# Filler work around 64 attention heads: from one generator with two calls per step to tasks placed by a planner

## The chip, the cores and the metric

The kernel runs on one core of a Trainium2 chip. The metric is the device time of one execution in microseconds (us). The core has TensorE (PE, matrix products and transposes into PSUM), VectorE (DVE), ScalarE (ACT), GpSimd (POOL) and SyncE (SP, which here issues the DMAs). Each engine works through its own instructions strictly in the order in which the program emits them, and an instruction waits on semaphores for operands that another engine makes.

## The reference

One layer of a hybrid backbone: 128 context tokens and 1024 latent tokens, model width 1024. Cut to what matters here:

```python
h = rmsnorm(x, norm1_w) * (1 + sc1) + sh1
aq, ak, av, mq, mk, mv, mo, mg = split(h @ w_in)      # 8 query heads, 2 key/value heads, 64 wide
attn_o = softmax(aq @ keys^T / 8) @ vals              # latent queries: 1024 latent + 128 context keys
hm = rmsnorm(mlstm(mq, mk, mv, gates)) * sigmoid(mo)
x = x + g1 * (concatenate([attn_o, hm]) @ w_out)
h2 = rmsnorm(x, norm2_w) * (1 + sc2) + sh2
g, u = split(h2 @ w_gu)                               # each 2816 wide
x = x + g2 * ((silu(g) * u) @ w_down)
y = rmsnorm(x, final_norm_w)
```

## The kernel before

The tokens stand in nine tiles of 128: tile `b = 0` is the context, `b = 1..8` are latent. The program has four stages, one after the other: modulation, first norm, input projection and the mLSTM heads; the attention stage; gate and up projection, in 22 pieces of 128 columns, with the down projection; the last norm. The change is all in the attention stage, which lies between about 437 and 838 us, and in the few microseconds after it.

**The attention stage** is a loop over `step(n)`, one step for each of 64 heads (8 latent tiles with 8 query heads), and some steps after the last head. The instructions of a head are spread over the engines, and in step `n`:

- PE computes the scores of head `n+2` into PSUM (`S<-kst,qT`, L1106; two halves of PSUM alternate, so they can only start once the exp of head `n` has read its half). On odd steps it also computes the values of the pair of heads that ended before (`po<-phT` and `po<-plT`, L1049, 18 products).
- DVE takes the reciprocal of head `n`'s sum (L1443) and scales it (L1444), finds the maximum of head `n+1` (`st<-S`, L1110), and makes the low half of head `n`'s probabilities (`pl`, L1454). Probabilities and weights are held as a high and a low half, so that two or three products give nearly f32.
- ACT makes the high half (`ph<-pr,st`, L1446), which needs DVE's scale, then the exp of head `n+1` (`pr<-S,st`, L1114), which needs DVE's maximum, and on odd steps copies the values out (`ol<-po`, L1054 and L1055).
- SP issues the transposing DMAs of both halves (L1450, L1455). POOL adds the two halves of the output (`oT`) and the gated residual (`x<-x,t`, L1132).

**The fillers** are all other work of this stage: the query projection of tiles 3 to 8 with its norm and rotary part (`q_part`), the turning of queries (`turn_products`, `turn_copies`), the splitting of `w_out` into a high and a low half (`out_load`, `out_split`), the mLSTM half of the output projection (`hm_part`), and the attention half with the second norm (`out_part`, `norm_stats`, `norm_rows`, `norm_turn`, `norm_out`). One piece of a projection (`out_block`, half a tile) is 12 products of 512 columns, and `add_gated` adds it to the residual `x1`. Before, one generator, `filler()`, walks through all of it in a fixed order, and a step calls it twice: the first `next(fill)` lets it emit a PE portion ahead of the values, the second, at the end of the step, the matching ACT and DVE instructions. So an ACT instruction and the DVE instruction that reads its result are emitted in the same step:

```python
def out_split(raw, tags):       # ACT cast, then DVE difference
    ...
    nc.scalar.copy(hi, raw)
    sub(lo, raw, hi.bitcast(F32), "dve")
```

After the last head come three more steps, the rest of the generator, and then the first gate/up piece, `pieces[0]`: its two 128x1024 weight tiles are loaded, measured (`measure`, L1522: a sum of squares on ACT), summed over the partitions (`scales`, one product with ones, L1527, and eight small DVE instructions), and split into two half-precision parts (`convert`: `wpair` on ACT, L1544, and its remainder on DVE, L1545). `split_down` does the like for `w_down`, piece by piece (`wdt`).

Of the kernel before, what the change touches and what calls it, by code (L numbers as in the profile page):

```python
# [19 lines left out]
P = 128  # L20
D = 1024
# [24 lines left out]
def hybrid_step(ctx: ExitStack, tc: tile.TileContext, I: dict, O: dict):  # L46
# [610 lines left out]
    def norm_rope_steps(qp, cc, ss, x, nb, nh, w, rb, eng=dve):  # L657
# [5 lines left out]
        act(sq, xf, AF.Square)  # L663
        ssum = qp.tile([P, 16], F32, name=nm("nrs"), tag="nrs", bufs=1)[:, :n]
# [358 lines left out]

    def turn_copies(b, ps):
        qT = qTs[b] = ap.tile([P, NQ, P], F32R, name=nm("qT"), tag="qT", bufs=2)
        psv = ps.rearrange("p (j x) -> p j x", j=4)
        qv = qT.rearrange("p (j g) x -> p j g x", g=2)
        for g in range(2):
            own = slice(64 * g, 64 * g + 64)
            far = slice(64 - 64 * g, 128 - 64 * g)  # L1030
            nc.scalar.copy(qv[own, :, g, :], psv[own])
            sub(qv[far, :, g, :], psv[own], qv[own, :, g, :].bitcast(F32), "dve")

    def new_oT(b):
        if b == 0:
            return half2[:, 5].rearrange("p (k x) -> p k x", k=4)
        if b in (3, 4):
            return hq.tile([P, 4, P], F32, name=f"o{b}")
        return ap2.tile([P, 4, P], F32, name=nm("oT"), tag="oT", bufs=3)
# [156 lines left out]
    def out_load(half, i):  # L1196
        n, j = divmod(i, 2)
        r0 = half * 512 + 2 * j * P
        raw = wp.tile([P, 1024], F32, name=nm("raw"), tag="raw", bufs=2)
# [25 lines left out]
    def q_part(state):  # L1225

        ropes = []
        raws, ws = [], []
        jobs = {1: lambda: raws.append(out_load(1, 0)), 2: lambda: raws.append(out_load(1, 1)),
                4: lambda: (ws.append(out_split(raws[0], ("wlo", "wlo"))), raws.append(out_load(1, 2))),  # L1230
                6: lambda: (ws.append(out_split(raws[1], ("wlo", "wlo"))), raws.append(out_load(1, 3))),
                8: lambda: ws.append(out_split(raws[2], ("wlo", "whi")))}
        s = 0
        for b in range(CB, NB):
            c, i = divmod(b, CB)
            sl = slice(i * P, (i + 1) * P)
            for half in range(2):
                if half == 0:
                    ps = bank()
                for k in range(4 * half, 4 * half + 4):  # L1240
                    wh, wl = w_q[k // 2]
                    ah, al = hTh[c][:, k, sl], hTl[c][:, k, sl]
                    mm(ps, ah, wh[:, k % 2, :], start=(k == 0), stop=False)
                    mm(ps, ah, wl[:, k % 2, :], start=False, stop=False)
                    mm(ps, al, wh[:, k % 2, :], start=False, stop=(k == KD - 1))
                yield 1
                if half == 1:
                    r = ev_rest(b, ps)
                    if r is not None:
                        ropes.append(r)  # L1250
                if ropes and next(ropes[0], ropes) is ropes:
                    ropes.pop(0)
                if s in jobs:
                    jobs[s]()
                s += 1
                yield
        while ropes:
            yield 0
            if next(ropes[0], ropes) is ropes:
                ropes.pop(0)  # L1260
            if len(ws) == 3:
                ws.append(out_split(raws[3], ("whi", "whi")))
            yield
        state["ws"] = [ws[0:2], ws[2:4]]

    def hm_part(ws):

        def load_hm(b):
            hm = t2()
            dma(hm, hm_d[b * P : (b + 1) * P, :])  # L1270
            return hm

        def load_x1(b):
            dma(x1[b], xrow(b))

        ring = [hq.tile([P, 2, 4, P], F32R, name=f"ring{i}") for i in range(2)]
        load_x1(0)
        hms = {0: load_hm(0)}
        raws = []
        for b in range(-1, NB):  # L1280
            for n in range(2):
                if b < 0 and n == 0:
                    continue
                if b >= 0:
                    th, tl = (ring[b % 2][:, t] for t in range(2))
                    ps = out_block(ws, n, th, tl)
                turn = b + 1 < NB and (n == 0 or b < 0)
                if turn:
                    pt = bank()
                    hm = hms.pop(b + 1)  # L1290
                    for j in range(4):
                        transpose(pt[:, j * P : (j + 1) * P], hm[:, j * P : (j + 1) * P])
                yield (b >= 0) + turn
                if b >= 0:
                    add_gated(x1[b], ps, gx[n] if b == 0 else gs[n], n, pool)
                if turn:
                    psv = pt.rearrange("p (j x) -> p j x", j=4)
                    oh, ol = (ring[(b + 1) % 2][:, t] for t in range(2))
                    nc.scalar.copy(oh, psv)
                    sub(ol, psv, oh.bitcast(F32), "dve")  # L1300
# [3 lines left out]
                    if b < 0:  # L1304
                        load_x1(1)
# [508 lines left out]
```

## Time and profile before

| quantity | value |
|---|---|
| median of 3 runs | 1655.72 us (1654.65 to 1659.19) |
| the profiled execution | 1659.14 us, its span 1657.4 us |
| mean granted clock of PE | 0.95 |
| PE busy | 1492.7 us, 90% of the span |
| DVE busy | 904.2 us, 55% |
| ACT busy | 734.2 us, 44% |
| POOL busy | 251.9 us, 15% |

The shares are of the whole span. In the page's row of 40 slices, each 41.4 us long, the attention stage lies in the 11th to the 21st, where PE's digits are 5, 8, 7, 9, 9, 8, 7, 8, 6, 6, 6 and those of the granted clock lie between 7 and 9; from the 22nd slice on PE stands at 9, with one 8 and a 5 in the last. Time in the stage is counted from head to head by the starts of `ph`, which ACT does once in each step.

### The profile page before, as it was taken

The numbers are of one execution on the slowest core, as the hardware profiler recorded it, in microseconds if no ns is written. First come the engines' busy times: TensorE is split into PE (matmuls) and PEld (weight loads), VectorE is DVE, ScalarE is ACT, GpSimd is POOL, SyncE is SP. The second block draws the span as 40 slices with busy tenths as digits, with TensorE's granted clock in tenths as the row PEclk, the third lists the DMA queues.
The fourth block names the chain that finished last, engine by engine and source line by source line (L and its number), as shares of the span: only waits on it lengthen the run. The fifth ranks groups of instructions, "written<-read, shape, count | busy, mean of one in ns | idle before, by whom it ended". The sixth has DMA issues, their size and how long they took to land.

```text
span 1657.4 us, 22938 instructions
## 1 busy us (share of the span) xinstructions
PE 1492.7 (90%) x8651; PEld 924.0 (56%) x8651; DVE 904.2 (55%) x2160; ACT 734.2 (44%) x1428; POOL 251.9 (15%) x272
## 2 busy tenths in 40 slices
PE   5899999898587998786669989999999999999995
PEld 1655666575354886665545555446664466655542
DVE  3844356749777787776654456333344332342278
ACT  3744343355475666787665556003250033422023
POOL 0411021313246333332210000000000000000001
PEclk8899999999797999887889999999999999999998
DMA  9345462301186988454557552431114410120223
GB/s 346 117 140 144 97 143 61 72 1 19 41 161 147 191 193 162 86 99 87 102 193 241 189 186 69 142 112 51 44 34 128 126 51 27 52 77 13 79 62 115
DMA packets 281829, 182.35 MB, mean 110 GB/s; under 512 B 167318, under 2 KB 253798, under 8 KB 281718
## 3 DMA queue, kind: packets, MB, share of 16 engines
q1 hardware_dynamic: 280294, 178.49, 41.5%
q10 hardware_dynamic: 1424, 2.40, 0.4%
q8 instruction: 68, 1.11, 0.3%
q14 instruction: 43, 0.35, 0.1%
HBM read 123.23 MB, written 19.29 MB: 86 GB/s over the span
## 4 chain that ended last, share of the span: by engine, by line
PE 37%; DMA 5%; DVE 4%; ACT 4%; issue 2%; POOL 1%; ACTq 0%; SPq 0%; DVEq 0%; POOLq 0%
PE mm L1176 8%; PE mm L1178 8%; PE mm L1177 8%; PE mm L1666 4%; PE mm L1667 4%; PE mm L1668 4%; DMA wdt<-in_w_down_dram 3%; DMA wd_d<-wdt 3%; DVE wdt L1501 1%; DVE x L1132 1%; ACT wdt L1495 1%; ACT wdt L1500 1%; DVE t L1131 1%; ACT jk L1522 1%; ACT jk L1752 0%
## 5 line engine op out<-in xcount | busy, mean ns | idle before, releaser
L1176 PE MATMUL mm<-h,wpair 128*128 128x384 f16 x1056 | 345.5, 327 | 6.0 <-ACT wpair L1544 6.0
L1177 PE MATMUL mm<-h,wpair 128*128 128x384 f16 x1056 | 345.6, 327 | 0.0
L1178 PE MATMUL mm<-h,wpair 128*128 128x384 f16 x1056 | 344.3, 327 | 0.0
L1629 DVE SCALAR_TENSOR_TENSOR tn<-tn,mm 128x384 f32<-128x384 f32 x66 | 36.4, 552 | 223.7 <-PE mm L1178 141.4
L1666 PE MATMUL mm<-wd,hl 128*128 128x512 f16 x396 | 149.9, 379 | 0.0
L1667 PE MATMUL mm<-wd,hl 128*128 128x512 f16 x396 | 149.9, 379 | 0.0
L1668 PE MATMUL mm<-wd,hl 128*128 128x512 f16 x396 | 149.6, 379 | 0.0
L1176 PEld LDWEIGHTS <-wpair 128*128 128x128 f16 x1056 | 105.5, 100 | 73.9 <-ACT wpair L1544 6.8
L1178 PEld LDWEIGHTS <-wpair 128*128 128x128 f16 x1056 | 103.4, 98 | 68.6 <-issue 0.5
L1177 PEld LDWEIGHTS <-wpair 128*128 128x128 f16 x1056 | 103.5, 98 | 67.0 <-issue 0.5
L1106 PE MATMUL S<-kst,qT 128*128 128x512 f32 (+1 forms) x384 | 96.6, 391 | 38.9 <-ACT pr L1114 37.1
L1755 POOL TENSOR_TENSOR x<-x,fw 128x512 f32<-128x512 f32 x9 | 11.5, 1277 | 770.2 <-ACT jk L1752 770.2
L499 PE MATMUL wi<-ipair,hT 128*128 128x384 f16 (+2 forms) x384 | 125.0, 326 | 2.8 <-ACT ipair L216 2.8
L1632 ACT ACTIVATE jk<-tn 128x384 bf16<-128x384 f32 x66 | 34.4, 521 | 208.9 <-DVE tn L1630 151.8
L501 PE MATMUL wi<-ipair,hT 128*128 128x384 f16 (+2 forms) x384 | 124.9, 326 | 0.5 <-POOL hT L135 0.5
L500 PE MATMUL wi<-ipair,hT 128*128 128x384 f16 (+2 forms) x384 | 125.0, 326 | 0.0
L1522 ACT ACTIVATE jk<-braw 128x1024 bf16<-128x1024 f32 x44 | 45.8, 1042 | 152.9 <-DVE x L1132 152.1
L1454 DVE SCALAR_TENSOR_TENSOR pl<-pr,st,ph 128x1152 f16<-128x1152 f32 x64 | 96.7, 1511 | 21.5 <-ACT ph L1446 19.6
L1446 ACT ACTIVATE ph<-pr,st 128x1152 f16<-128x1152 f32 x64 | 80.2, 1253 | 55.0 <-issue 38.2
L1106 PEld LDWEIGHTS S<-kst,qT 128*128 128x128 f32 x384 | 68.8, 206 | 60.8 <-ACT pr L1114 48.0
L1110 DVE TENSOR_REDUCE st<-S 128x1 f32<-128x1152 f32 x64 | 86.6, 1353 | 28.0 <-PE S L1106 27.6
L1131 DVE SCALAR_TENSOR_TENSOR t<-mm,gm,gl 128x512 f32<-128x512 f32 x64 | 47.6, 744 | 81.3 <-PE mm L1668 81.3
(423 smaller groups left out, 2867.4 us busy)
## 6 DMA issues: line engine op xcount, KB each, us to landing
wd<-wd_d SPq DMA_DIRECT2D x58, 512.0 KB
braw<-in_w_gu_dram SPq DMA_DIRECT2D x44, 512.0 KB
a4s<-in_w_ada_dram SPq DMA_DIRECT2D x32, 512.0 KB
wdt<-in_w_down_dram SPq DMA_DIRECT2D x22, 512.0 KB
wd_d<-wdt SPq DMA_DIRECT2D x22, 512.0 KB
x<-in_x_sample_dram SPq DMA_DIRECT2D x17, 512.0 KB
aw<-in_w_ada_dram SPq DMA_DIRECT2D x16, 512.0 KB
iraw<-in_w_in_dram SPq DMA_DIRECT2D x32, 256.0 KB
```

Source lines behind the costliest of these rows:

```text
L499: mm(ps[:, :n], ah, wh[:, k % 2, c0 : c0 + n], start=(k == 0), stop=False)
L500: mm(ps[:, :n], ah, wl[:, k % 2, c0 : c0 + n], start=False, stop=False)
L501: mm(ps[:, :n], al, wh[:, k % 2, c0 : c0 + n], start=False, stop=(k == KD - 1))
L1106: mm(S[:, lo:hi], qTs[b][:, h, :], kst[kv][:, t, lo:hi], start=(t == 0), stop=(t == 1))
L1110: dve.tensor_reduce(out=stat[n][:, 0:1], in_=score[n], axis=AX.X, op=ALU.max, negate=True)
L1176: mm(ps, wh[:, k, :], th[:, k, :], start=(k == 0), stop=False)
L1177: mm(ps, wh[:, k, :], tl[:, k, :], start=False, stop=False)
L1178: mm(ps, wl[:, k, :], th[:, k, :], start=False, stop=(k == KD - 1))
L1454: dve.scalar_tensor_tensor(out=pl, in0=pr, scalar=st[:, 3:4], in1=ph, op0=ALU.mult, op1=ALU.subtract)
L1666: mm(ps, ah, w[:, k, 0], start=(j + k == 0), stop=False)
L1667: mm(ps, ah, w[:, k, 1], start=False, stop=False)
L1668: mm(ps, al, w[:, k, 0], start=False, stop=(j + k == g["nf"] - 1))
```

## The change

The generator is replaced by a class `Filler` that holds tasks. A task is a generator that yields, ahead of each portion, the engine that it is for, a cost in us, a lag (how many steps after the task's portion before it the portion may come; 1 unless stated), the number of PSUM banks that it takes, and a condition. At each step every engine gets a credit (PE 3.5, ACT 1.9, DVE 2.0 us, held at most at 1.5 times that), and `run(engine)` emits portions while the credit is positive. Portions of lag 0 on ACT and DVE are emitted last in the step ("behind"). After the last head the credits are 5.0.

```diff
+    class Filler:
...
+        def run(self, engine, behind=False):
+            order = sorted((t for t in self.tasks if t[1][0] == engine), key=lambda t: t[1][1])
+            for task in order:
+                while task[1] is not None:
+                    want, cost, lag, need, ready = task[1] + (0.0, 1, 0, None)[len(task[1]) - 1 :]
+                    if want != engine or self.step - task[2] < lag or need > self.banks or behind != (lag == 0 and engine != "X"):
+                        break
+                    if not behind and self.credit.get(engine, 1.0) <= 0.0 or ready is not None and not ready():
+                        break
...
+    fl = Filler(PE=3.5, ACT=1.9, DVE=2.0)
...
+    def w_task(half, i, tags, load=None, ready=None):
+        yield "X", 0.0, 0, 0, load
+        raw = out_load(half, i)
+        stamp(("raw", half, i))
+        yield "ACT", 1.05, 2, 0, ready
+        hi, lo = (wp.tile([P, 1024], F32R, name=nm(t), tag=t, bufs=5) for t in tags)
+        nc.scalar.copy(hi, raw)
+        yield "DVE", 1.2
+        sub(lo, raw, hi.bitcast(F32), "dve")
...
+    def hm_task(b):
+        yield "X", 0.0, 0, 0, lambda: fl.step >= 4 if b == 0 else since(("hmT", b - 1), 0)
+        hm = t2()
+        dma(hm, hm_d[b * P : (b + 1) * P, :])
+        dma(x1[b], xrow(b))
...
+    def mix_task(b):
...
+            yield "DVE", 0.7, 0
+            add_gated(x1[b], ps, gx[n] if b == 0 else gs[n], n, pool)
+            fl.free()
+        yield "ACT", 1.25, 1
+        w = norm_stats(b)
+        yield "DVE", 2.0
+        rs[b] = rsqrt1(w, 1.0 / D)
+        if b == NB - 1:
+            return
+        yield "ACT", 1.35, 1, 0, lambda: b == 0 or ("turned", b - 1) in at
+        ys = norm_rows(b)
+        yield "PE", 1.5, 1, 2
+        pss = norm_turn(ys)
...
+    def first_piece():
+        p = pieces[0]
+        yield "X", 0.0, 0, 0, lambda: ("normed", 3) in at
+        p.load()
+        for j in range(2):
+            yield "ACT", 1.25, 2
+            p.measure((j,))
+        yield "PE", 0.1, 1, 1
+        yield "DVE", 1.4, 0
+        p.scales()
+        fl.free()
+        for j in range(2):
+            yield "ACT", 1.05
+            p.convert((j,))
+            fl.credit["DVE"] -= 1.2
+        stamp("piece")
...
     def step(n):
...
-        used = next(fill, 0)
...
+        fl.run("PE")
...
-        next(fill, None)
-        if turn:
-            turn_copies(b + 1, ps)
...
+        fl.run("X")
+        for behind in (False, True):
+            for e in ("ACT", "DVE"):
+                fl.run(e, behind)
+        fl.run("X")
...
-    pieces[0].load()
-    pieces[0].measure()
-    pieces[0].scales()
-    pieces[0].convert()
```

Beside these, `norm_out` becomes `norm_mod` (the first half of a tile's scaling all on ACT, the second all on DVE, before two and two of each half) and `norm_split`; tiles 3, 4 and 5 of the attention output lie in `q_rest`; the fourth `w_out` load of the second half uses the tile `fl`; the pools of the later stage open in a task of their own. The products and the other instructions are the same in kind and almost in number. In the changed program the lines are some 4 to 60 further on (`ph` is L1509, `pr` L1118, `pl` L1517).

How the instructions move is shown at three places. The first is the split of a `w_out` portion early in the stage. On ACT, before, the cast to `wlo_5124` stands at the end of a step, behind the value copies `ol` and ahead of the next head's `ph`:

```order
L1114 ACTIVATE pr_5091,st_5089<-S_4796,st_5089 128x1152
L1054 ACTIVATE ol_5095<-po_4797,vsc 64x256
L1055 ACTIVATE ol_5095<-po_4797,vsc 64x256
L1205 CAST wlo_5124<-raw_4971 128x1024
L1446 ACTIVATE ph_5168<-pr_5091,st_5089 128x1152
L1114 ACTIVATE pr_5174,st_5172<-S_4796,st_5172 128x1152
```

On DVE, before, the difference that reads `wlo_5124` stands in the same step, ahead of the reciprocal and the scale of `st_5089` for which that `ph` waits:

```order
L131 SCALAR_TENSOR_TENSOR ry_5101<-rt_5102,ry_5101 128x16
L135 TENSOR_TENSOR wlo_5125<-raw_4971,wlo_5124 128x1024
L1443 RECIPROCAL st_5089<-st_5089 128x1
L1444 TENSOR_SCALAR st_5089<-st_5089 128x1
L1110 TENSOR_REDUCE st_5172<-S_4796 128x1
L1454 SCALAR_TENSOR_TENSOR pl_5169<-pr_5091,st_5089,ph_5168 128x1152
```

So ACT's `ph` stood behind a DVE instruction that itself stood behind ACT. On ACT, after, two casts of `w_out` portions are emitted in one step:

```order
L1509 ACTIVATE ph_5000<-pr_4953,st_4951 128x1152
L1118 ACTIVATE pr_5008,st_5006<-S_4796,st_5006 128x1152
L1327 CAST wlo_5012<-raw_4918 128x1024
L1327 CAST wlo_5015<-raw_4920 128x1024
L1509 ACTIVATE ph_5057<-pr_5008,st_5006 128x1152
L1118 ACTIVATE pr_5063,st_5061<-S_4796,st_5061 128x1152
```

On DVE, after, their two differences come a step later, behind `pl_5058`:

```order
L1517 SCALAR_TENSOR_TENSOR pl_5001<-pr_4953,st_4951,ph_5000 128x1152
L1506 RECIPROCAL st_5006<-st_5006 128x1
L1507 TENSOR_SCALAR st_5006<-st_5006 128x1
L1114 TENSOR_REDUCE st_5061<-S_4796 128x1
L1517 SCALAR_TENSOR_TENSOR pl_5058<-pr_5008,st_5006,ph_5057 128x1152
L135 TENSOR_TENSOR wlo_5013<-raw_4918,wlo_5012 128x1024
L135 TENSOR_TENSOR wlo_5016<-raw_4920,wlo_5015 128x1024
L1506 RECIPROCAL st_5061<-st_5061 128x1
```

What moved is the DVE half: it no longer stands between the cast and the scale of the head that follows it.

The second place is the first gate/up piece, whose tiles are named `wpair`. On PE, before, the last output block (`mm_8212<-...,kst`) is followed by the product with ones and then by the first gate/up products:

```order
L1138 MATMUL mm_8212<-whi_6632,kst_4270 128x512
L1139 MATMUL mm_8212<-whi_6633,kst_4270 128x512
L1140 MATMUL mm_8212<-whi_6632,kst_4271 128x512
L1527 MATMUL mm_8251<-fv_8246,ones 128x2
L1176 LDWEIGHTS wpair_8261
L1176 MATMUL mm_8295<-h_1292_6898,wpair_8261 128x384
```

On PE, after, the last block is followed by the turning of a norm's rows `y` (of tile 7) and at once by the first gate/up products:

```order
L1142 MATMUL mm_8206<-whi_6781,kst_4270 128x512
L1143 MATMUL mm_8206<-whi_6782,kst_4270 128x512
L1144 MATMUL mm_8206<-whi_6781,kst_4271 128x512
L114 MATMUL mm_8226<-ident,y_8219 128x128 x4
L114 MATMUL mm_8231<-ident,y_8221 128x128 x4
L1180 LDWEIGHTS wpair_7955
L1180 MATMUL mm_8291<-h_1334_7140,wpair_7955 128x384
```

The product with ones is now within the steps. So is the split, `wpair_7955` and `wpair_7999`, on ACT, after, in the steps of heads 60 and 61:

```order
L1118 ACTIVATE pr_7946,st_7944<-S_4796,st_7944 128x1152
L1058 ACTIVATE ol_7950<-po_4797,vsc 64x256
L1059 ACTIVATE ol_7950<-po_4797,vsc 64x256
L1600 ACTIVATE wpair_7955<-braw_7634,fv_7717 128x1024
L1509 ACTIVATE ph_7987<-pr_7946,st_7944 128x1152
L1118 ACTIVATE pr_7993,st_7991<-S_4796,st_7991 128x1152
L1419 CAST kst_4270<-oT_7431 128x512
L1600 ACTIVATE wpair_7999<-braw_7636,fv_7717 128x1024
```

The remainder of each `wpair` on DVE is emitted in the step of its ACT part, as on DVE, after, for the second of them:

```order
L1517 SCALAR_TENSOR_TENSOR pl_7988<-pr_7946,st_7944,ph_7987 128x1152
L1601 SCALAR_TENSOR_TENSOR wpair_7999<-braw_7636,fv_7717,wpair_7999 128x1024
L1506 RECIPROCAL st_7991<-st_7991 128x1
L1507 TENSOR_SCALAR st_7991<-st_7991 128x1
L1114 TENSOR_REDUCE st_8026<-S_4796 128x1
```

So this one split still stands, on DVE, ahead of the scale of the following head.

The third place is the next piece of gate/up on ACT, after: its parts `wpair_8403` and `wpair_8406` come behind two `tn` (the nonlinearity of the first piece's products `mm_8291` and `mm_8377`) and behind a `wdt` split:

```order
L1713 ACTIVATE tn_8369<-mm_8291,fv_7717 128x384
L1551 ACTIVATE wdt_8278<-wdt_8278,wds 128x2x512
L1551 ACTIVATE wdt_8280<-wdt_8280,wds 128x2x512
L1717 ACTIVATE jk_8373,gst_8287<-tn_8369 128x384
L1713 ACTIVATE tn_8452<-mm_8377,fv_7717 128x384
L1600 ACTIVATE wpair_8403<-braw_8274,fv_8318 128x1024
L1600 ACTIVATE wpair_8406<-braw_8276,fv_8318 128x1024
```

Before, both of the first two pieces were measured together after the last block; now only the second is, and its split follows the first piece's products.

More of the change, by code (lines that the diff above doesn't have):

```diff
@@ L1223, in hybrid_step @@
     h2 = H2()
[L1225 to L1264, printed above, removed]
@@ new lines, in turn_task @@
+    def turn_task(b):
+        yield "PE", 0.7, 1, 1, lambda: (b < CB or since(("rope", b), 2)) and fl.step >= 8 * (b - 2) + 1
+        ps = turn_products(b)
+        yield "ACT", 1.2
+        qT, psv, qv = turn_tile(b, ps)
+        for own, far, g in turn_halves():
+            nc.scalar.copy(qv[own, :, g, :], psv[own])
+        yield "DVE", 1.4
+        for own, far, g in turn_halves():
+            sub(qv[far, :, g, :], psv[own], qv[own, :, g, :].bitcast(F32), "dve")
+        fl.free()
+        qTs[b] = qT
@@ new lines, in hm_task @@
+    def hm_task(b):
[3 more added lines that the diff above has]
+        dma(x1[b], xrow(b))
+        yield "PE", 0.7, 2, 1, lambda: b == 0 or since("pools", 2) and (b < 3 or ("hmO", b - 2, 1) in at)
+        ps = bank()
+        for j in range(4):
+            transpose(ps[:, j * P : (j + 1) * P], hm[:, j * P : (j + 1) * P])
+        stamp(("hmT", b))
+        th, tl = ring[2 - b % 2 if b > 0 else 0]
+        psv = ps.rearrange("p (j x) -> p j x", j=4)
+        yield "ACT", 0.6, 0
+        nc.scalar.copy(th, psv)
+        yield "DVE", 0.7
+        sub(tl, psv, th.bitcast(F32), "dve")
+        fl.free()
+        for n in range(2):
+            yield "PE", 2.9, 1, 1, lambda: since(("w", 1, 2 * n + 1)) and since(("w", 1, 2 * n))
+            ps = out_block(w_of(1), n, th, tl)
+            stamp(("hmO", b, n))
+            yield "DVE", 0.7, 0
+            add_gated(x1[b], ps, gx[n] if b == 0 else gs[n], n, pool)
+            fl.free()
+        stamp(("hm", b))
@@ L1406, in filler, with pools_task @@
[L1406 to L1420 removed]
+    def pools_task():
+        yield "X", 0.0, 0, 0, lambda: since(("rope", NB - 1), 0)
+        open_pools()
+        stamp("pools")
@@ L1462, in step @@
             late[:] = []
-        next(fill, None)
-        if turn:
-            turn_copies(b + 1, ps)
-    pairs, late = {}, []
-    fill = filler()
-    with tc.manual_schedule(engines=ENGINES):
-        head_scores(0)
-        head_scores(1)
-        head_max(0)
-        head_exp(0)
-        n = 0
-        while n < len(heads) + 3:
-            step(n)
-            n += 1
-        for _ in fill:
-            pass
+        fl.run("X")
[3 more added lines that the diff above has]
+        fl.run("X")
     def split_down():
```

299 lines of the change are left out of this document (167 added, 132 removed).

## Prediction

> **What bounds the kernel now.** I cut the span into stages by the table of busy times over windows (us, then busy time and count of PE, its weight loads, DVE, ACT and POOL, then PE's granted clock, the DMA share and GB/s).
>
> ```profile
> 544.00:629.00 85.00, 83.96 (x475) 68.99 (x473) 68.00 (x93) 55.38 (x77) 28.71 (x33) 1.00 0.90 191
> 675.00:730.00 55.00, 44.67 (x231) 35.04 (x230) 39.48 (x85) 40.18 (x66) 20.62 (x22) 0.88 0.50 92
> 821.00:850.00 29.00, 13.02 (x68) 9.69 (x66) 8.67 (x34) 15.62 (x30) 7.85 (x9) 0.79 0.54 165
> 850.00:1005.00 155.00, 147.25 (x888) 88.53 (x889) 79.10 (x207) 92.36 (x155) 2.32 (x2) 0.97 0.60 200
> 1005.00:1600.00 595.00, 595.00 (x3349) 327.53 (x3348) 225.19 (x467) 151.91 (x301) 0.00 (x0) 1.00 0.24 71
> ```
>
> From 1005 us on PE is never idle, and from 850 to 1005 it lacks 7.75 us of being full. The products there don't change, so nothing is to be had but those 7.75 us. From 544 to 629, sixteen heads (16 to 31), PE is busy 83.96 of 85 us: it bounds. In the other parts of the attention stage no engine is full (675 to 730: 44.67 us of 55 on PE, 40.18 on ACT, 39.48 on DVE), so there the steps wait for each other. The time of the stage is that between the first and the last `ph`, which the line's own view gives:
>
> ```profile
> L1446 ACT ACTIVATE ph<-pr,st x64: 1238/1256/1258, 445.1 to 820.7; 128x1152 f16<-128x1152 f32 x64
> ```
>
> That is 375.6 us for 63 steps, 5.96 a step. The view of waits between 445 and 850 us (who waited for what: total, times, longest) says for what:
>
> ```profile
> ACT ph L1446 <- issue: 38.2, 24, 4.7
> PE S L1106 <- ACT pr L1114: 34.2, 23, 4.4
> DVE t L1129 <- PE mm L1140: 23.6, 14, 10.9
> ACT pr L1114 <- DVE st L1110: 22.8, 19, 2.2
> ACT y L1339 <- DVE r L1192: 19.2, 8, 3.1
> ACT ph L1446 <- DVE st L1444: 13.3, 11, 1.5
> ```
>
> "Issue" stands where the profile names no releaser. The timeline of ACT (two rows) and DVE (two) shows what it is at one of the 24 places:
>
> ```profile
> 484.17 1.03 ACT L1205 CAST wlo<-raw 128x1024 fp32r<-128x1024 f32 x1
> 486.94 1.26 ACT L1446 ACTIVATE ph<-pr,st 128x1152 f16<-128x1152 f32 x1 [1.73 <-issue]
> ...
> 485.24 1.35 DVE L135 TENSOR_TENSOR wlo<-raw,wlo 128x1024 fp32r<-128x1024 f32 x1 [1.97 <-ACT wlo L1205]
> 486.51 0.15 DVE L1443 RECIPROCAL st<-st 128x1 f32<-128x1 f32 x1
> ```
>
> DVE idles 1.97 us until ACT has cast, then subtracts for 1.35 us; only then come reciprocal and scale, and the scale is what ACT's next `ph` needs, and ACT idles 1.73 us. In such a step the two engines work one after the other. `y<-r` is the same the other way round: the norm's small DVE chain and the ACT scaling that reads it are in one step.
>
> **The change part by part.** The sums are made against the profiled execution, 1659.1 us; the median of the runs is 3.4 us lower, which I take off at the end.
>
> *A. The steps, head 0 to head 63.* Instructions neither vanish nor come in number; what changes is in which step they stand. From the order of both programs I counted each step's portions, with these durations (busy, mean ns, idle before; the PE rows are starts):
>
> ```profile
> L1454 DVE SCALAR_TENSOR_TENSOR pl<-pr,st,ph 128x1152 f16<-128x1152 f32 x64 | 96.7, 1511 | 21.5 <-ACT ph L1446 19.6
> L1110 DVE TENSOR_REDUCE st<-S 128x1 f32<-128x1152 f32 x63 | 85.2, 1353 | 28.0 <-PE S L1106 27.6
> L1114 ACT ACTIVATE pr<-S,st 128x1152 f32<-128x1152 f32 x63 | 76.6, 1217 | 23.4 <-DVE st L1110 22.8
> L1360 ACT ACTIVATE fl<-mm,shift2s,scale2s 128x128 f32<-128x128 f32 x32 | 11.9, 448 | 0.0
> L1339 ACT ACTIVATE y<-x,r 128x512 f32<-128x512 f32 x16 | 10.7, 714 | 19.2 <-DVE r L1192 19.2
> ...
> 599.94 1.35 PE L1106 MATMUL S<-kst,qT 128*128 128x512 f32 x6
> 601.13 0.45 PE L1138 MATMUL mm<-wlo,ring 128*128 128x512 f32 x1
> 603.93 0.60 PE L114 MATMUL mm<-ident,q_rest 128*128 128x128 f32 x4
> 604.37 0.27 PE L1049 MATMUL po<-phT,vs 128*128 128x256 f16 x1
> 604.47 0.27 PE L1049 MATMUL po<-plT,vs 128*128 128x256 f16 x1
> ```
>
> So PE takes 1.2 us for a head's scores, 2.8 for an output block (601.13 to 603.93), and 0.11 for each of the 18 value products of a pair. In the changed program heads 20 and 21 have on PE 1.2 + 2.8 and 1.2 + 2 x 2.8 + 2.0 us, 12.8 for the pair, where before they had 10.6. I take the busiest of PE, ACT and DVE for each pair of heads, because PE runs two heads ahead and evens out single steps, and add them up: before 327 us, after 336. The planner's order is by itself 9 us worse, nearly all from heads 56 on (29.0 to 38.1), into which the first piece's measuring, splitting and scaling moves: on ACT two sums and two halves of 1.2 and 1.1 us each, on DVE two of 1.3 and eight small ones. Over heads 0 to 55 the sums are equal, 298 us.
>
> What the trace shows beyond the sum is 375.6 - 327 = 48.6 us, and none of it lies in heads 16 to 31, where the sum is the time. The two waits that the lags take away, `ph<-issue` and `y<-r`, are 57.4 us, more than the whole 48.6 (some of it lies where PE would have bound anyway). What stays: `add_gated` still follows its block in the step (lag 0), 23.6 us less the 10.9 and the 2.1 us of the two last ones, which come after the heads, is 10.6; and `convert` still puts ACT's half and DVE's remainder into one step, two times 1.73. Together 14 us. A is then 336 + 14 - 375.6 = -25.6 us. Ends: with nothing staying beyond the sum -39.6; with all 48.6 staying +9. I take the first value since the coupling is seen at its place in the rows, and since heads 16 to 31 reach their sum as soon as it is absent.
>
> What is late next: `pr<-st` and `ph<-st`, 36.1 us, the chain within a head; they stay, and are cost only where PE has no lead.
>
> *B. From the last `ph` to the last output block.* Rows of ACT and PE in time:
>
> ```profile
> 828.82 0.47 ACT L1054 ACTIVATE ol<-po,vsc 64x256 f32<-64x256 f32 x1 [2.46 <-PE po L1049]
> 837.87 0.40 PE L1140 MATMUL mm<-whi,kst 128*128 128x512 f32 x1
> 840.44 1.06 ACT L1331 ACTIVATE jk<-x 128x1024 bf16<-128x1024 f32 x1 [8.98 <-POOL x L1132]
> 843.72 0.59 PE L1527 MATMUL mm<-fv,ones 128*128 128x2 f32 x2 [5.45 <-ACT jk L1522]
> 848.95 2.17 ACT L1544 ACTIVATE wpair<-braw,fv 128x1024 f16<-128x1024 f32 x2
> 850.14 0.50 PE L1176 MATMUL mm<-h,wpair 128*128 128x384 f16 x1 [5.83 <-ACT wpair L1544]
> ```
>
> Now ACT has two `y`, eight `fl`, four casts and two `ol` between the last `ph` and the last `ol`: 1.4 + 3.6 + 2.5 + 1.0 = 8.5 us from 822.0 on, to 830.5 instead of 828.8 (before, ACT idled 2.46 us there). That is +2 us, between 0 (the values come as late) and +3.
>
> *C. From the last block to gate/up.* PE idles from 838.3 to 850.14, 11.9 us, while ACT waits for the residual, measures four tiles, and splits. With `wpair` made within the steps PE goes on at once with the turning of tile 7's rows, 1.3 us (not new work, only moved behind the block). Gate/up then starts 10.6 us earlier, but piece 1 is split behind the second `tn` and behind `wdt`, so PE waits about 3 us ahead of piece 1: behind the first piece's last product come `tn` (0.6), two halves of `wpair` (2.2, from the row above) and a remainder on DVE (1.3), and PE has 1.3 us of its own to cover them. C is -11.9 + 1.3 + 3 = -7.6; ends -10.6 and 0.
>
> Sum: -25.6 + 2 - 7.6 = -31.2, 1627.9 us, and with the 3.4 taken off 1624.5 us.
>
> **A rule weighed.** PE's granted clock falls in idle time. The following rows show how soon:
>
> ```profile
> 723.33 1.27 PE L114 MATMUL mm<-ident,y 128*128 128x128 f32 x8 [2.40 <-ACT y L1339]
> 725.12 0.42 PE L1049 MATMUL po<-plT,vs 128*128 128x256 f16 x1
> 725.33 0.42 PE L1049 MATMUL po<-phT,vs 128*128 128x256 f16 x1
> ```
>
> After a gap of 2.40 us the value products come to stand 0.21 us apart instead of 0.11, so a gap of that size may halve the rate; rival 1 rests on this. [...]
>
> **The rivals.**
>
> *1. The clock.* The planner leaves PE idle for 1 to 3 us in many steps that were full: in heads 16 to 31 the pairs sum to 79 us with only 68 of PE. Nine pairs from head 8 to 59, 93 us, are still PE's. At the clock of 0.88 of the row from 675 to 730 they stretch by 93 x (1/0.88 - 1) = 13 us: 1637. For it: that row, with 44.67 us of PE in 55. Against: only where PE is the longest does its clock cost anything.
>
> *2. The loss stays in part.* Half of the 48.6 us is the chain within a head after all (36.1 us of waits speak for it). A is 336 + 24.3 - 375.6 = -15.3 and the time 1634.8; if all stays, A is +9, the sum +3.4 and the time 1659: no gain. Against: heads 16 to 31.
>
> *3. The tail comes back.* Between 850 and 1005 us the chain that ended last runs through the splitting of `w_down`, whose first tiles can only load once the last block is through:
>
> ```profile
> 838.50 4.42 DMA wdt<-in_w_down_dram
> 1002.39 2.09 ACT jk L1522 x4
> ```
>
> If it sets the time, an earlier gate/up only makes PE idle 7.75 + 7.6 us there, C is 0, and the time 1632. Against: only four gaps, of 7.75 us in all, show PE waiting for it.
>
> *4. Slower, by SP.* The mLSTM tiles' loads stand in SP's queue between the transposes of the heads:
>
> ```profile
> 539.09 0.57 SPq L1270 DMA_DIRECT2D t<-hm_d  x1
> 539.71 0.43 SPq L1274 DMA_DIRECT2D x<-in_x_sample_dram  x1
> 541.50 1.49 SPq L1450 DMA_TRANSPOSE phT<-ph  x1
> ```
>
> Each now is issued as soon as the tile before is turned, and must have one of three buffers that ACT's measures and `add_gated` use too. If it waits for one, the transposes behind it wait, then the values, then `ol`. To turn -31.2 into +5 each of the nine loads would have to hold the steps up by 4 us; at 5 us each A is -25.6 + 45 = +19.4, the sum +13.8, and the time 1669.5. Against: before, with the same buffers, the row shows the two loads 0.6 us apart and heads 16 to 31 lose nothing.
>
> **How the numbers follow.** My forecast (A between -14 and -39.6) has 0.50, 1610 to 1637. Rival 1 has 0.09, rival 2 0.18 (of it 0.06 with no change), rival 3 0.09, rival 4 0.08, and a larger gain (PE evening out more than pairs, A to -57, the sum of the longer of ACT and DVE alone being 318.6 us) 0.06. A measurement of this kernel can tell 0.3%, 5 us, from no change. Faster: 0.50 + 0.09 + 0.12 + 0.09 + 0.06 = 0.86; the same 0.06; slower 0.08. The range ends at 1603, short of the larger gain, and at 1650, where A is nothing and B and C are as forecast (1659.1 - 5.6 - 3.4).
>
> **What would show it.** The starts of `ph` 350 us apart from first to last; `ph<-issue` under 10 us and `y<-r` near 0; DVE waiting for ACT's `wlo` and `ring` no more; PE at 1.00 of its clock between heads 16 and 31 or, for rival 1, at 0.8 to 0.9 there; the gap ahead of the first gate/up product under 2 us, one of about 3 us ahead of piece 1 and not more than 8 us of idle PE after it; SP's loads of `hm` without waits. I am wrong if the heads take over 365 us with those waits gone: then the chain within a head was the bound.

## The result and the profile after

The changed kernel takes 1644.93 us (median of 6 runs, 1640.41 to 1648.71) against 1655.38 us before (6 runs, 1654.61 to 1659.19): 0.9932 of the time before, 95% interval 0.9911 to 0.9953. It is faster by 10 us, where 31 were forecast. The profiled execution took 1645.31 us, its span 1643.5; that of before lies 3.8 us above its median, so the two spans differ by more than the medians.

The view of one line for `ph`, which now is L1509, in the changed kernel:

```profile
L1509 ACT ACTIVATE ph<-pr,st x64: 1239/1256/1260, 443.0 to 805.9; 128x1152 f16<-128x1152 f32 x64
```

ACT's waits between 443 and 806 us (total, times, longest), of the changed kernel:

```profile
ACT ph L1509 <- issue: 59.6, 27, 4.9
ACT pr L1118 <- DVE st L1114: 24.8, 22, 3.2
ACT nr L663 <- POOL q_rest L687: 7.8, 1, 7.8
```

The heads take 362.9 us instead of 375.6. The wait of `y` for the norm's chain is gone from the list (it was 19.2 us), but `ph<-issue`, expected under 10 us, has grown to 59.6. And there is one wait of 7.8 us that was not there.

The order of time between the last `ph` and gate/up in the changed kernel, for PE and for what it waits for on POOL, DVE and ACT:

```profile
811.89 2.26 POOL L135 TENSOR_TENSOR h<-fl,h 128x512 f16<-128x512 f32 x2
814.19 1.37 DVE L1453 TENSOR_SCALAR fl<-mm,scale2s,shift2s 128x128 f32<-128x128 f32 x4 [4.27 <-POOL h L135]
815.61 0.80 PE L1142 MATMUL mm<-wlo,kst 128*128 128x512 f32 x1 [4.67 <-DVE fl L1453]
823.43 0.47 ACT L1058 ACTIVATE ol<-po,vsc 64x256 f32<-64x256 f32 x1 [6.57 <-PE po L1053]
834.02 0.40 PE L1144 MATMUL mm<-whi,kst 128*128 128x512 f32 x1
837.45 0.32 PE L1180 MATMUL mm<-h,wpair 128*128 128x384 f16 x1 [1.46 <-DVE fl L1453]
```

Gate/up starts 3.0 us behind the last block instead of 11.9. But a block of tile 7 stands ahead of the last pair's values and waits 4.67 us for a PSUM bank, which DVE's `fl` clears; `fl` waits 4.27 us for POOL, which still reads tile 5's values out of the one `fl` buffer, while this `fl` is tile 6's. So the last values come out at 823.4 us, 17.5 us behind the last `ph` (before: 8.1).

Where the 13.9 us between the two spans lie:

| stretch | before | after | difference | forecast |
|---|---|---|---|---|
| to the first `ph` | 445.1 | 443.0 | -2.1 | 0 |
| A, first to last `ph` | 375.6 | 362.9 | -12.7 | -25.6 |
| B, last `ph` to the end of the last block | 17.6 | 28.5 | +10.9 | +2 |
| last block to gate/up | 11.9 | 3.0 | -8.8 | C, with the next row: -7.6 |
| from gate/up to the end of the span | 807.3 | 806.1 | -1.2 | |

### The profile page after: what moved, and what is told of

It is laid out like the page before. It is cut to its first block, busy times and chain, and to the rows that moved or that the text cites. A ratio compares the mean times of both kernels' runs of the same rounds, so it can differ in the third digit from the quotient of the medians.

```text
span 1643.5 us, 22904 instructions
## 1 busy us (share of the span) xinstructions
PE 1489.5 (91%) x8651; PEld 921.1 (56%) x8651; DVE 902.0 (55%) x2160; ACT 732.4 (45%) x1428; POOL 251.1 (15%) x272
## 4 chain that ended last, share of the span: by engine, by line
PE 37%; DMA 5%; DVE 4%; ACT 4%; issue 1%; POOL 0%; ACTq 0%; SPq 0%; DVEq 0%; POOLq 0%
PE mm L1180 8%; PE mm L1182 8%; PE mm L1181 8%; PE mm L1751 4%; PE mm L1752 4%; PE mm L1753 4%; DMA wd_d<-wdt 3%; DMA wdt<-in_w_down_dram 2%; DVE x L1136 1%; ACT wdt L1546 1%; DVE wdt L1552 1%; ACT wdt L1551 1%; DVE t L1135 1%; ACT jk L1576 0%; ACT jk L1837 0%
## 5 line engine op out<-in xcount | busy, mean ns | idle before, releaser
L1517 DVE SCALAR_TENSOR_TENSOR pl<-pr,st,ph 128x1152 f16<-128x1152 f32 x64 | 95.1, 1486 | 31.9 <-ACT ph L1509 29.0
L1509 ACT ACTIVATE ph<-pr,st 128x1152 f16<-128x1152 f32 x64 | 80.3, 1254 | 68.0 <-issue 59.6
```

What stands on the lines that cost most here:

```text
L1517: dve.scalar_tensor_tensor(out=pl, in0=pr, scalar=st[:, 3:4], in1=ph, op0=ALU.mult, op1=ALU.subtract)
```

## The experiments

Each run is compared with the kernel before on the same chip. All are in this table: the three stretches of the profiled execution (A, B, and the gap from the last block to gate/up), their sum, and the ratio to before with its 95% interval. The sum tells of the attention stage; the ratio has also the spread of what follows: from gate/up to the end of the span, which the changes don't touch, it is 803.3 us in the profile of `e2_before_early_scale` and 815.2 in that of `e5_scale_and_max_early`. The last two runs leave keys of the odd heads out; all others compute everything.

| run | A | B | gap | sum | ratio |
|---|---|---|---|---|---|
| before | 375.6 | 17.6 | 11.9 | 405.1 | |
| after | 362.9 | 28.5 | 3.0 | 394.4 | 0.9932 (0.9911 to 0.9953) |
| e7_lag_zero | 399.2 | 20.5 | -0.2 | 419.5 | 1.0096 (1.0058 to 1.0134) |
| e13_before_norm_lag | 361.0 | 18.4 | 12.8 | 392.2 | 0.9921 (0.9902 to 0.994) |
| e14_before_split_lag | 372.2 | 19.1 | 11.9 | 403.2 | 0.9981 (0.9967 to 0.9995) |
| e10_before_lag | 353.5 | 21.1 | 12.8 | 387.4 | 0.9896 (0.9853 to 0.994) |
| e16_before_three_lags | 380.9 | 23.4 | 12.8 | 417.1 | 1.0074 (1.0057 to 1.009) |
| e9_before_first_piece | 383.4 | 21.4 | -0.2 | 404.6 | 1.0034 (1.0016 to 1.0052) |
| e11_planner_without_piece | 353.6 | 24.9 | 12.8 | 391.3 | 0.9952 (0.9934 to 0.9969) |
| e3_square_later | 362.0 | 28.4 | 3.0 | 393.4 | 0.9947 (0.9927 to 0.9968) |
| e4_values_first | 365.7 | 25.6 | 3.0 | 394.3 | 0.9948 (0.9928 to 0.9968) |
| e12_two_mends | 359.7 | 25.3 | 3.0 | 388.0 | 0.9911 (0.9878 to 0.9945) |
| e15_planner_mends_no_piece | 356.0 | 24.5 | 12.8 | 393.3 | 0.9942 (0.9919 to 0.9965) |
| e8_one_block_a_step | 361.7 | 33.0 | 4.8 | 399.5 | 0.997 (0.9946 to 0.9993) |
| e1_early_scale | 364.7 | 28.2 | 4.8 | 397.7 | 1.0008 (0.999 to 1.0026) |
| e2_before_early_scale | 372.5 | 19.1 | 11.9 | 403.5 | 1.0013 (0.9992 to 1.0034) |
| e5_scale_and_max_early | 366.9 | 28.8 | 3.0 | 398.7 | 1.0023 (1.0007 to 1.004) |
| e6_before_scale_and_max | 394.1 | 19.2 | 12.9 | 426.2 | 1.013 (1.0096 to 1.0165) |
| e17_own_banks | 362.2 | 27.1 | 3.0 | 392.3 | 0.9931 (0.9907 to 0.9956) |
| e18_lags_own_banks | 353.5 | 21.0 | 12.8 | 387.3 | 0.9886 (0.9861 to 0.9911) |

The heads of `e4_values_first` are the same program as those of the changed kernel and took 2.8 us longer, so differences of 3 us in A tell nothing.

**Is the lag what gains?** Taken out of the planner's pairs:

```diff
         nc.scalar.copy(hi, raw)
-        yield "DVE", 1.2
+        yield "DVE", 1.2, 0
```

and the same for the mLSTM tile, the turned tile and the rotary sum. The norm's chain keeps its lag in this run. Portions of lag 0 are emitted at the end of the step whatever credit is left, so portions move as well.

> The changed kernel, with the lag taken out of the pairs: DVE's difference for a w_out split, an mLSTM tile and a turned query tile, and the sum of the rotary part, may follow their ACT half at the end of the same step, as before. If the lag is what the planner gains by: the heads go from 363 to 375 us or more. If a lag gains nothing because ACT and DVE go step by step together (a pair that is parted costs the longer engine in two steps): the heads stay within 5 us of 363, and the time within 5 us of the changed kernel. The sum of each step's longest engine is 4 to 6 us more than in the changed kernel, since PE's portions come in other steps too.

The heads took 399.2 us, 36 more than with the lags and 24 more than before. So the planner's packing without these lags is worse than the order written out by hand. But the 36 us are not the pairs' alone: 26.0 of them lie in heads 16 to 31 (108.3 us against 82.3), where the order of before, with such pairs in one step, took 85.4. ACT's longest waits during the heads:

```profile
ACT ph L1509 <- issue: 76.5, 34, 4.6
ACT pr L1118 <- DVE st L1114: 37.5, 25, 5.6
ACT ph L1509 <- DVE st L1507: 7.6, 7, 2.7
```

The timelines of ACT tell how much of the idle time ahead of `ph` comes directly behind ACT's half of one of these four kinds of pairs: before, 37 us of 55; in the changed kernel, 10 of 68; in this run, 37 of 87. So the waits that the lags were meant to take away did go. In the changed kernel 32 of the 68 us come directly behind the exp, where ACT had no portion at all and waited for the other engines.

**The lag alone, in the order of before.** A step of its own for the norm's chain, and DVE's `w_out` differences run at the end of the next step (the loads that follow them move along):

```diff
-                    norms[0] = (b, 2, norm_rows(b, what))
+                    rs[b] = rsqrt1(what, 1.0 / D)
+                    norms[0] = (b, 2, None)
+                elif stage == 2:
+                    norms[0] = (b, 3, norm_rows(b))
...
-        sub(lo, raw, hi.bitcast(F32), "dve")
+        pend.append(lambda: sub(lo, raw, hi.bitcast(F32), "dve"))
```

> The kernel before, its generator in the same order, with a lag alone: DVE's difference of a w_out split comes at the end of the next step, and the norm's small DVE chain has a step of its own ahead of the ACT scaling that reads it. In the trace of before these two kinds of pairs stand behind 7.4 us of waits of ph and 19.2 us of waits of y. If lags pay by the waits they take away: heads 10 to 20 us shorter (355 to 366). If each step lasts as its longest engine and parting a pair only spreads it over two steps: less than 5 us. The last norm comes a step later, which may lengthen the end by up to 2 us.

Heads of 353.5 us, 22.1 under before and level with the planner that is left without the first piece (353.6, below); 0.9896 of the time, the fastest of the runs that compute everything. Its interval overlaps with that of the changed kernel, so the two are not told apart by the time. Then each part of it:

> The kernel before, with the lag of the norm's small DVE chain alone (a step of its own ahead of the ACT scaling). Both lags together gave heads of 353.5 us against 375.6 and 0.9896 of the time. If the gain follows the waits (y waits 19.2 us of the 26.6): heads 357 to 362 us, 0.990 to 0.994. If a wait taken away here is given back (the longest engine of the step binds anyway): heads 366 us or more, above 0.996.

> The kernel before, with the lag of the w_out splits alone (DVE's difference at the end of the next step). If the gain follows the waits (7.4 us of ph behind eight pairs): heads 366 to 371 us, 0.995 to 0.999 of the time. If these pairs are what holds the early steps (heads 4 to 15 and 30 to 36): heads under 364 us, below 0.994.

For the norm's chain the gain follows the waits: 14.6 us for 19.2 of `y`. The 3.4 us of the splits are at the edge of what A can tell, though the time fell too (0.9981, below 1 with its whole interval). The expectation counted 7.4 us for them; in the timeline of before `ph` waits 15.6 us directly behind the casts of seven splits, and 5.7 with the lag. But its whole idle time fell only from 55.0 to 50.5 us, so most of that wait came back at other places. With the norm's lag, in the waits of ACT during the heads, no `y` is left, and yet `ph<-issue` is larger than before (38.2):

```profile
ACT ph L1448 <- issue: 54.3, 28, 7.2
ACT pr L1114 <- DVE st L1110: 18.7, 17, 2.2
ACT ph L1448 <- DVE st L1446: 16.2, 12, 2.8
```

A third lag, `yield` behind the rotary part's Square, didn't tell what it was for:

```diff
         act(sq, xf, AF.Square)
+        yield
```

> The kernel before with the two lags, and a third: a step between the rotary part's Square on ACT and DVE's sum over it. If the gain follows the waits (12.6 us in heads 4 to 13): heads 343 to 348 us against 353.5, the time 0.983 to 0.987. If it is given back (the rotary part takes a step more for each pair of tiles, so that all that follows comes later, and POOL's buffer holds up the next Square): heads 352 us or more, 0.989 or more.

The heads went up by 27 us, mostly the last 31 (heads 32 to 63: 194.6 us against 171.0 with two lags). All fillers behind the rotary part come at other steps, and how they then fall on the steps with and without values wasn't tried by itself, so this run is inconclusive on the third lag.

**The first piece alone, and the planner without it.**

```diff
+        if n in (57, 59):
+            pieces[0].measure(((n - 57) // 2,))
...
+        if n in (61, 62):
+            pieces[0].convert((n - 61,))
```

> The kernel before, its generator unchanged, with only the first gate/up piece moved into the steps: loaded in step 55, measured in 57 and 59, scaled in 60, split in 61 and 62. If the gain of the change is this part (the idle PE between the last block and gate/up, 11.9 us before and 3.0 after) and the planner as a whole gains nothing: heads longer by 2 to 4 us, the gap shorter by 8 to 10, the time 5 to 9 us under before, as much as the changed kernel has or nearly. If the planner is what gains: at most 3 us under before.

```diff
-        fl.add(first_piece())
...
+    pieces[0].load()
+    pieces[0].measure()
+    pieces[0].scales()
+    pieces[0].convert()
```

> The changed kernel, with the first gate/up piece measured and split after the heads as before; the planner with its budgets and lags stays. If the planner gains nothing over heads and end together (before 375.6 + 17.6 = 393.2 us, after 362.9 + 28.5 = 391.4): the gap ahead of gate/up is 10 to 13 us again and the time 1650 to 1656, no better than before. If the heads gain by having less to do (their last eight from 44 to 39 us): part of it comes back, the time 1645 to 1650.

In the order of before the gap of 11.9 us went to nothing, but the heads grew by 7.8 and B by 3.8 us: sum 404.6 against 405.1, and the time didn't fall. In the planner the same piece costs 9.3 us of heads and 3.6 of B for 9.8 of the gap. Moving it into the steps gains nothing in the sum of either, and the intervals of the two planner runs overlap; both expectations had it as a gain.

**The two new stalls.** ACT's row in the changed kernel, and POOL's that it waits for; they share the buffer `nr`:

```profile
495.36 2.34 POOL L687 TENSOR_TENSOR q_rest<-q_rest,nr 128x1024 f32<-128x1024 f32 x1
497.73 1.06 ACT L663 ACTIVATE nr<-q_rest 128x1024 f32<-128x1024 f32 x1 [7.83 <-POOL q_rest L687]
```

The Square is held until two steps after the rotary part of the tile two before it:

```diff
-        yield "ACT", 1.1, 0, 0, lambda: b - 2 < CB or ("rope", b - 2) in at
+        yield "ACT", 1.1, 0, 0, lambda: b - 2 < CB or since(("rope", b - 2), 2)
```

> The changed kernel, with the rotary part's Square on ACT held until two steps after the former rotary part was issued (one condition), so that it no longer waits on ACT for POOL to be through with the buffer they share. If the 7.8 us stall at head 8 (ACT idle from 489.9 to 497.7 us) is a plain loss: the heads shrink by 6 to 8 us, the time to 1637 to 1639. If PE or DVE are the bound there and only take it up: under 2 us.

In the step behind the last head PE's portions come after the value products:

```diff
-        fl.run("PE")
+        if n < len(heads):
+            fl.run("PE")
...
+        if n >= len(heads):
+            fl.run("PE")
```

> The changed kernel, with PE's values put ahead of PE's portions in the steps after the last head. If the 10.9 us that the end lost (last ph to last output block: 28.5 us against 17.6) come from the values of the last pair standing behind a block that waits for a PSUM bank: last ph to last block falls to 18 to 22 us and the time by 6 to 10 us. If the clock (products 0.43 us apart instead of 0.23 there) or the copies of the values are what is slow: under 3 us.

Both together, and then both without the first piece:

> The changed kernel with both mends that were tried apart: the Square held until POOL is through, and the values ahead of PE's portions after the last head. Apart they measured 0.9947 and 0.9948 of before where the changed kernel has 0.9932, so neither is told from it. If they add up where the profile shows them (0.9 us of the heads, 2.9 us of the end): 3 to 5 us under the changed kernel, 0.990 to 0.992 of before. If the runs' own spread of 8 us is all there is: 0.993 to 0.995.

> The planner with the first piece after the heads as before, the Square held until POOL is through, and the values ahead of PE's portions after the last head. If packing by budgets costs nothing beyond its two stalls: heads 349 to 353 us, last ph to last block 21 to 23, 0.988 to 0.992, level with the lag alone (0.9896). If it costs: 0.993 or more.

With the Square held two steps the wait fell to 4.0 us and heads 0 to 7 from 55.6 to 48.1 us, but heads 8 to 15 rose from 46.4 to 51.0: most of it was taken up. Values ahead of the fills brought B down by 2.9 us, not 6: the last values came out 6.5 us earlier, but ACT's copy of them for the last two blocks then waited 3.85 us for POOL, whose sum `oT` stood behind tile 7's gated residual. Both mends together lie 6 us lower in the sum; the interval reaches that of the changed kernel. Without the first piece they don't come below the lag alone (393.3 against 387.4).

**Bursts.** At most one PE portion of over 2 us in a step:

```diff
+                    if engine == "PE" and cost > 2.0 and self.step < 64:
+                        if big:
+                            break
+                        big = 1
```

> The changed kernel, with at most one PE portion of over 2 us (half of a query tile's projection or one output block) in a step while heads remain. Burst theory (two in one step hold up the scores, the next maximum and add_gated behind them): the heads fall by 6 to 12 us from 363, those of heads 0 to 7 from 55.6 to under 50. If bursts are evened out by the lead of two heads: the heads change by less than 3 us. The blocks that no longer fit come after the last head and lengthen the end by up to 6 us.

Heads 0 to 7 fell to 46.2 us as expected, but heads 8 to 15 have a wait of 13.7 us, and the total hardly moved. PE and DVE there:

```profile
499.88 1.11 PE L114 MATMUL mm<-ident,q_rest 128*128 128x128 f32 x4 [7.46 <-POOL q_rest L687]
509.20 1.36 DVE L1114 TENSOR_REDUCE st<-S 128x1 f32<-128x1152 f32 x1 [13.65 <-PE S L1110]
```

PE itself stands for POOL's rotary part with all its later work behind it. B grew to 33.0 us by the blocks that no longer fit. So bursts cost in the first heads, and the same microseconds came back elsewhere.

**Are ACT and DVE tied by the scale that stands behind DVE's portions?** That was my first theory of the missing 13 us. Each head's scale is taken in the step before it, behind `pl` and ahead of DVE's portions, in the changed kernel and in the kernel before (first two runs); then the next maximum too (the last two lines of the diff):

```diff
             dma_t(two_n[1][:, h % 2, :, :], pl)
+            if n + 1 < len(heads):
+                head_scale(stat[n + 1])
+            if n + 2 < len(heads):
+                head_max(n + 2)
```

> The changed kernel, with one thing moved: DVE's reciprocal and scale of head n+1 are emitted in step n right behind pl of head n and ahead of DVE's portions of that step, instead of at the start of step n+1 behind them. Lockstep theory (ACT's ph waits for the scale, which stands behind DVE's portions, so that each step lasts as long as the longer of ACT and DVE): the idle time before ph put down to issue falls from 59.6 us to under 25, the heads (first to last ph) from 362.9 us to 343 to 352, and the time from 1645 to 1625 to 1635. Rival, the burst theory (two output blocks of PE in one step delay the scores, and nothing else is lost): the heads stay within 5 us of 362.9 and the waits only move from ph to pr, the exp.

> The kernel before, with the same single move of reciprocal and scale ahead of DVE's second call of the generator. Lockstep theory: the 32 us that its heads last beyond the sum of each step's longest engine (375.6 against 343) are mostly that lock, so the heads fall by 15 to 25 us, to 351 to 361, and the time to 1631 to 1641, with no planner at all. Burst theory: there are no bursts here (one block in a step), so the loss before was the cast-difference pairs only; with the scale ahead of them they matter less, 5 to 10 us.

> The changed kernel, with the scale of head n+1 and also the maximum of head n+2 emitted in step n right behind pl of head n, ahead of DVE's portions of that step. Moving the scale alone only moved the wait from ph (67 to 10 us) to the exp (25 to 85 us), which waits for the maximum that stands behind the same portions. Lockstep theory, now with both: ACT's idle time before ph and exp falls from 92 us to 50 to 65, the heads from 363 us to 340 to 352, the time by 10 to 20 us against the changed kernel. Rival (PE sets the steps: the maximum now needs the scores a step sooner, and DVE waits for PE instead): DVE's idle time before the maximum rises from 39 to over 60 us, the heads stay at 358 us or more.

> The kernel before, with the same two moves. Lockstep theory: heads from 375.6 us to 350 to 362, the time by 12 to 25 us under before. Rival (PE): heads 370 us or more, the time within 5 us of before.

None gained. The wait went from `ph` to the exp, first behind the maximum, then behind PE's scores (ACT's longest wait during the heads, with the scale alone, then with both):

```profile
ACT pr L1118 <- DVE st L1114: 85.1, 42, 5.4
```

```profile
ACT pr L1118 <- PE S L1110: 78.8, 40, 5.6
```

So the tie isn't one instruction's place. The last row led to PE: in the changed kernel the maximum of head 23 waits for scores that are not its own. The scores of odd heads begin with a product of 512 columns, those of even heads with one of 128 (PE, PE, DVE):

```profile
568.85 1.37 PE L1110 MATMUL S<-kst,qT 128*128 128x512 f32 x6
577.46 1.41 PE L1110 MATMUL S<-kst,qT 128*128 128x128 f32 x6
578.91 1.36 DVE L1114 TENSOR_REDUCE st<-S 128x1 f32<-128x1152 f32 x1 [2.12 <-PE S L1110]
```

Head 23's scores were through at 570.2; its maximum starts behind head 24's, at 578.9. The program emits the scores of head `n+2` ahead of the maximum of head `n+1`. The odd heads' half of `S2` ends at column 1151 and the even heads' begins at 1408, so both write into the columns 1024 to 1535, one bank of 512 as the program counts them (`bank()`). In the next two runs the odd heads write nothing there:

```diff
+                to = S[:, 896:1024] if n % 2 and lo == 1024 else S[:, lo:hi]
+        if n % 2:
+            score[n] = bc(S2[:, 0:576], 1, [P, 2, 576])
```

> The changed kernel, where odd heads no longer use the shared bank: their last 128 keys' scores are written over columns 896 to 1023, and maximum and exp read columns 0 to 575 twice instead of 1152 columns once. So the odd heads' result leaves keys out; every instruction is there with its size. If the shared bank ties head n+1's maximum to the scores of head n+2, so that PE has a lead of one head only: DVE's idle time before the maximum falls from 39 us to under 15, the heads from 363 us to 340 to 352, the time by 8 to 20 us. If a head's own scores are what the maximum waits for: the heads stay within 4 us of 363.

> The kernel before with its two lags, with the same change of the odd heads (it too leaves keys out of them). If the shared bank holds PE's lead to one head: heads from 353.5 us to 332 to 346, DVE's idle time before the maximum from 27 us to under 10, the time 0.975 to 0.985 of before. If not: heads 350 us or more, 0.988 to 0.991.

A is the same to 0.7 us in both, and DVE waits as it did, at the same place for 2.12 us (the place in the run with banks apart):

```profile
573.92 1.36 DVE L1117 TENSOR_REDUCE st<-S 128x1 f32<-128x1152 f32 x1 [2.12 <-PE S L1111]
```

So the wait for the next head's scores is there, and the shared bank is not its cause. In the kernel before and in the changed one no maximum starts until the scores of the next head are through; in both the earliest starts 0.03 us behind their end. Of the 63 that have a next head, 30 in the kernel before and 44 in the changed one start within 0.2 us of that end. In `e5` and `e6`, where the maximum is emitted ahead of those scores, it starts up to 7 us before they end (in `e5` a maximum at 577.14), and there it is the exp, emitted behind them, that never starts until they are through (at 584.18 there, after 5.61 us of waiting for PE's scores). So in these runs an instruction that reads one half waited for the scores that were emitted ahead of it into the other. The program holds both halves in one tile, `S2`; that its waits go by the tile would fit, but a tile for each half wasn't tried, so this last step stays open.

## Why the prediction was wrong, point by point

**A, the base of the sum: the step that failed.** I added up the longest engine for pairs of heads "because PE runs two heads ahead and evens out single steps". By single steps, with the same durations, the changed kernel's sum is 350 us, where I had 336, and that of before about 341, where I had 327. So 14 us of what I took for loss lay in the steps themselves, and no lag takes them out. With 350 in place of 336 my sum gives A as -11.6; measured -12.7. That it comes so near is partly luck: the heads took 362.9, which is 350, the one POOL wait of 7.8 and 5 us, and that wait was not among the 14 us that I let stay. In about half of its 63 steps the trace is within 0.5 us of the step's longest engine. Why PE's lead doesn't even out is seen at the maxima, none of which starts until the scores of the head after are through: PE's lead is one head shorter than I took it. That single steps are the right sum is a fit to this trace; in the order of before it falls short by 35 us, which is where the pairs stand.

**A, the lag.** Forecast -34.6 us (48.6 of loss down to 14). Two kinds of pairs parted in the order of before gave -22.1. Four kinds joined again in the planner cost 36.3, of which 26.0 lie in heads 16 to 31, where the order of before has such pairs too and took 85.4 us against 108.3. The two runs share only the `w_out` splits, so neither number measures the forecast's term. That the waits go is shown (`y` from 19.2 us to nothing, `ph` behind the pairs from 37 to 10); the size of 34.6 is not. The first piece's share, forecast as 9 us (29.0 to 38.1), measured 9.3. What packing costs by itself isn't told apart: without the piece, the planner with all its lags and the order of before with two of them have the same heads (353.6 and 353.5).

**B** was forecast as +2, from ACT's instructions alone, and measured +10.9. I had not counted the queue on PE: a block of tile 7 ahead of the last values, waiting for a bank, behind DVE, behind POOL. Three output blocks come after the last `ph`, where before had two, and the products of the first of them stand 0.43 us apart instead of 0.23. Of the 10.9, 3.6 go without the first piece, 2.9 with the values first, and 4.0 with both (`e15`, which also holds the Square), so 6.9 stay unexplained by a run.

**C** was forecast as -7.6 and came out at -10.0 (-8.8 and -1.2, the latter well within the spread of what follows gate/up). The wait of 3 us ahead of piece 1 didn't come: in the list of PE's waits after the gap only the sums over partitions are left, 8.0 us against 7.4 before. So the chain of `w_down` took nothing back, and rival 3 is out.

**The rivals.** Rival 1, the clock, had 0.88 over heads 16 to 31. Windows of the kernel before over heads 32 to 39, then of the changed kernel over heads 16 to 31 and over 32 to 39 (columns as before, the granted clock third from the end):

```profile
629.00:675.00 46.00, 36.92 (x177) 27.98 (x176) 34.17 (x53) 34.31 (x51) 16.31 (x18) 0.89 0.70 131
545.00:628.00 83.00, 72.48 (x401) 58.09 (x401) 63.27 (x86) 55.17 (x77) 34.33 (x35) 0.96 0.83 180
628.00:671.00 43.00, 40.16 (x219) 31.70 (x218) 34.72 (x47) 29.01 (x40) 13.19 (x15) 1.00 0.87 161
```

Over heads 16 to 31 the clock fell from 1.00 only to 0.96, with PE idle for 10.5 us, and over heads 32 to 39 it rose from 0.89 to 1.00. Idle time alone did not set it: from 671 to 713 us of the changed kernel PE was idle for 6.0 us, and the clock stood at 1.00. So the rival is out. Rival 2, that half of the loss stays, gave A as -15.3, near the -12.7 that came, though not by its reason. Rival 4 didn't come: heads 16 to 31, with the mLSTM loads in SP's queue, took 82.3 us against 85.4. The signs that I named were met by `y<-r` and the gap ahead of gate/up, and failed by `ph<-issue`, which is no measure of loss: it rose in the two kernels with shorter heads too (54.3 us with the norm's lag and 47.0 with both lags in the order of before).

## What to carry to other kernels

When engines pass a head through in step, add up the longest engine of each single step, unless a row of the trace shows one of them working ahead (here 350 of 362.9 us, where pairs of steps gave 336); for each queue ask which work of the step before it truly waits for. Where an engine's own loop instruction stands behind a small instruction that waits for another engine, one step between the two can gain most of the wait without repacking, as it did for the norm's chain (14.6 of 19.2 us). It is not sure to: the splits gained 3.4 us where `ph` had waited 15.6 behind them, and a third lag, which also moved all work behind it, cost 27. Before a planner's order is believed, look at what POOL and the single buffers hold at the places where work is drawn together.

## What the runs showed of the hardware

After the 4.67 us gap PE's output products stood 0.43 us apart instead of 0.23 (815.61 on). In the last two blocks, which began behind a gap of 2.74 us and had one of 0.62 us more, they began at 0.23 and changed to 0.43 only 2.4 us after the start, for about 3 us:

```profile
827.82 0.39 PE L1142 MATMUL mm<-whi,kst 128*128 128x512 f32 x1
828.05 0.40 PE L1143 MATMUL mm<-whi,kst 128*128 128x512 f32 x1
829.00 0.63 PE L1143 MATMUL mm<-wlo,kst 128*128 128x512 f32 x1
829.43 0.63 PE L1144 MATMUL mm<-wlo,kst 128*128 128x512 f32 x1
832.16 0.39 PE L1142 MATMUL mm<-wlo,kst 128*128 128x512 f32 x1
832.39 0.40 PE L1143 MATMUL mm<-wlo,kst 128*128 128x512 f32 x1
```

So the slower rate came at once behind the long gap and late behind the short ones; whether one of the short ones brought it isn't told apart. In the kernel before, the last two blocks began behind a gap of 2.81 us and had one of 0.62 us more too, and their products stood 0.23 to 0.24 us apart from then to their end (833.21 to 837.87). What length of gap brings the slower rate, if it is the gap, these runs don't show.
